# Two requests of 64 partitions in place of one with an outermost dimension of two, for the queries and keys of an attention head

## The chip, the cores and the metric

The kernel runs on one core of a Trainium2 chip. The metric is the device time of one execution in microseconds (us). The core has five engines with a queue of instructions each: PE (TensorE, the matrix products), DVE (VectorE), ACT (ScalarE), POOL (GpSimd) and SP (SyncE). A DMA request is an instruction in the queue of the engine that issues it, here SP or ACT; the bytes are then moved by the core's 16 DMA engines.

## The reference

One layer over 2048 latent tokens on a grid of 32 x 64 and 256 context tokens, width 1024. Shown is what the change touches: every latent query reads a window of 8 x 16 grid cells, with a learned bias, and all 256 context keys in one softmax.

```python
h_lat = _rmsnorm(x, norm_g[i]) * (1.0 + scale) + shift
na_q, na_k, na_v, na_g, r_q, r_k, r_v, r_g = _split_proj(h_lat @ w_in)
...
s_loc = jnp.einsum('bhrqd,bhrkd->bhrqk', qr, kg, preferred_element_type=jnp.float32) * scale + bias[None]
s_loc = jnp.where(mask, s_loc, -jnp.inf)
s_ctx = jnp.einsum('bhrqd,bhcd->bhrqc', qr, k_ctx, preferred_element_type=jnp.float32) * scale
p = jax.nn.softmax(jnp.concatenate([s_loc, s_ctx], axis=-1), axis=-1)
...
o = jnp.einsum('bhrqk,bhrkd->bhrqd', p_loc, vg) + jnp.einsum('bhrqc,bhcd->bhrqd', p_ctx, v_ctx)
```

There are 8 attention heads of width 64. Four retention heads of width 128 (a chunked recurrence in both directions) use the other columns of the projection. Both groups are gated, concatenated, projected by `w_out`, added to `x` and normalised.

## The kernel before

The products are made exact with pairs: a float32 tile is split into a high part `hi` (the reduced type that PE takes at speed) and a low part `lo`, and three products hi-hi, lo-hi and hi-lo are summed. That is why queries and keys exist twice in memory.

The work runs in four stages, in the order that the program writes out by hand for each engine.

1. Until about 165 us: normalisation of the tokens and projection of the attention keys. The keys of a pair of heads go to the DRAM tensor `kS`, with shape 128 x 2 x 2304 (64 rows for each head, the high and the low copy, the tokens).
2. Until about 597 us: the projections that are a list of jobs. `run_jobs` takes a block of 256 weight columns at a time and runs units over it. At the start of a job it splits the next job's weights (`w_parts`, ACT line 336, POOL line 338) and has SP load the weights after that (line 175). The value units `u_v` (nine for each of two jobs) copy a result of 256 tokens into a staging tile `o`, of which there are two, and store it into `vB` in eight requests of 24 or 32 partitions. The query units write `qS`, with shape 4 x 128 x 2 x 512 for each pair of heads: a block of 512 queries, 64 rows for each head, high and low copy.
3. Until about 1390 us: attention. A tile is a head with 128 queries; 8 heads with 4 blocks of 4 tiles make 128 tiles. The loop is a pipeline over four tiles: scores of tile t (`s_mm`, line 753, PE), normalisation of t-1, transposes of t-2 (`p_tr`), products with the values of t-3 (`pv`). Between these, `fill` deals out steps of the remaining projections, 318 of 384 over the loop, so that each tile gets between two and three.
4. The retention and the output projection.

Scores are computed with one instruction for 128 rows of the array: queries in rows 0 to 63 and the same queries again in rows 64 to 127, keys' high part in rows 0 to 63 and low part in rows 64 to 127. So both loads fill 128 partitions from 64 rows of memory. The query load repeats 64 rows twice; the key load takes the high and low copy from the middle dimension:

```python
for hl in range(2):
    nc.tensor.matmul(o, hd["q"][i][:, hl, j * P:(j + 1) * P], k, start=(hl == 0), stop=(hl == 1))
```

The query load (`load_q`, line 725) is issued by ACT, at the first tile of the block before; there are two query tiles. The key load (`load_head`, line 717) is issued by SP in the second block of the head before; there are two key tiles. Values (`load_v`, line 732), bias (line 737) and the weights of the filling projections (line 175) are SP's requests too, in the order of the program; a request whose buffer isn't free holds back those behind it. ACT also issues the gate loads (line 814) and all stores through `store`, which `defer` puts off until the next `tick`, the end of a unit or of a tile.

Of the kernel before, what the change touches and what calls it, by code (L numbers as in the profile page):

```python
# [81 lines left out]
def hybrid_kernel(ctx: ExitStack, tc: tile.TileContext, a: dict, out: bass.AP):  # L82
    nc = tc.nc
    f = lambda ap: ap[:].bitcast(F32)
# [3 lines left out]
    kS = [dram.tile([P, 2, LT], F32, name=f"kS{t}") for t in range(4)]  # L88
# [47 lines left out]
    def defer(n, fn):  # L136
        later.append([n, fn])
# [9 lines left out]
    def store(dst, src, n=1):  # L147
        q = env["queue"]
        defer(n, lambda: q.dma_start(dst, src))
# [211 lines left out]
    def tokform(w, tp):  # L361
        pm = ptile()
        for t in range(2):
            tk = 2 * tp + t
            (h1, h0), o = blk[tk // 4], (tk % 4) * P
            for k in range(KC):
                for i, (h, ww) in enumerate(((h1, w[0]), (h0, w[0]), (h1, w[1]))):
                    nc.tensor.matmul(pm[:, t * WG:(t + 1) * WG], h[:, k, o:o + P], ww[:, k, :],  # L368
                                     start=(k == 0 and i == 0), stop=(k == KC - 1 and i == 2))
                if k % 2 == 1:  # L370
                    yield
        return pm
# [45 lines left out]
    def u_v(w, c0, tp):  # L418
        pm = yield from tokform(w, tp)
        vt = op.tile([P, 2, 2, 2, P], F32R, name="o")  # L420
        pv = pm.rearrange("p (t h e d) -> p t h e d", t=2, h=2, e=2)
        for e in range(2):
            hs, ls = slice(64 * e, 64 * e + 64), slice(64 - 64 * e, 128 - 64 * e)
            nc.scalar.copy(vt[:, :, :, e, hs], pv[:, :, :, e, :])
            nc.vector.tensor_tensor(vt[:, :, :, e, ls], pv[:, :, :, e, :], f(vt)[:, :, :, e, hs], ALU.subtract)
        s, o = (c0 - 1024) // WG, f(vt).rearrange("p t h e d -> p t (h e d)")
        if tp == 8:
            store(vS[s].rearrange("(t p) h d -> p t (h d)", p=P), o)
            return
        for e, j in enumerate(VORD):  # L430
            k0, cw = CWIN[j]
            dst = vB[s][:4 * cw, tp, e, :].rearrange("(t r c) d -> r c t d", t=2, r=2)
            for r in range(2):
                store(dst[r], o[64 * r + k0:64 * r + k0 + cw])

    def put_tok(dstt, c0, tp, r, n=1):
        store(dstt[(c0 % 512) // WG][tp * 256:(tp + 1) * 256, :].rearrange("(t p) d -> p t d", p=P), r, n)
# [52 lines left out]
    run_acts(-1)  # L490

    jobs = [(1024, [(u_v, (tp,)) for tp in range(9)]), (1280, [(u_v, (tp,)) for tp in range(9)])]
    jobs += [(c0, [(u_gate, (ct, b)) for ct in range(2) for b in range(4)]) for c0 in (1536, 1792)]
    for n, (c0, u) in enumerate(((2560, u_rk), (2816, u_rk), (3072, u_rv), (3328, u_rv))):
# [219 lines left out]

    def load_head(h):
        k2 = kp.tile([P, LT], F32R, name="k2")
        nc.sync.dma_start(f(k2), kS[h // 2][64 * (h % 2):64 * (h % 2) + 64].rearrange("p e t -> e p t"))
        vc = kp.tile([P, 2, P], F32R, name="vc")
        nc.sync.dma_start(f(vc), vS[h // 4][:, h % 4, :].rearrange("(n p) d -> p n d", p=P))
        return dict(k2=k2, h=h, vc=vc, vt={}, q={})  # L720

    def load_q(hd, h, i):
        q = kp.tile([P, 2, 512], F32R, name="q", bufs=2)
        src = qS[h // 2][i, 64 * (h % 2):64 * (h % 2) + 64]
        nc.scalar.dma_start(f(q).rearrange("p e t -> p (e t)"), src.rearrange("p e t -> p (e t)").unsqueeze(0).to_broadcast([2, 64, 1024]))
        hd["q"][i] = q

    def load_v(hd, gs):
# [12 lines left out]
    def dims(t):  # L741
        h, i, j = t // 16, t // 4 % 4, t % 4
        return h, i, j, KWIN[i][0], KWIN[i][1], CWIN[j][0], CWIN[j][1]
# [90 lines left out]
    def run(n):  # L834
        for un in qu[n:n + 1]:
            for _ in un:
                pass
            tick()

    heads[0] = load_head(0)  # L840
    load_q(heads[0], 0, 0)
    load_v(heads[0], (0, 1, 2))
    for n in range(4):
# [118 lines left out]
    for t in range(NT + 3):  # L962
# [27 lines left out]
        h, i, j = dims(t)[:3]  # L990
# [7 lines left out]
        if i < 3 and j == 0:  # L998
            load_q(hd, h, i + 1)
        for g in {(0, 2): (3,), (0, 3): (4,), (1, 1): (5,), (1, 3): (6,), (2, 3): (7,)}.get((i, j), ()):  # L1000
            load_v(hd, (g,))
        if h + 1 < NH:
            if i == 1 and j == 2:
                heads[h + 1] = load_head(h + 1)
            if i == 3:
                nh = heads[h + 1]
                if j == 0:
                    load_q(nh, h + 1, 0)
                if j == 1:
                    bias(h + 1, 0, 0)  # L1010
                    load_v(nh, (0,))
                if j == 3:
                    bias(h + 1, 0, 1)
                    load_v(nh, (1, 2))
# [213 lines left out]
    q, r = divmod(48 - used, 7)  # L1228
    plan = [q + (n < r) for n in range(7)] + [15] * 8 + [10] * 4
    for s in range(NJ + 3):  # L1230
        q = plan[s]
# [121 lines left out]
```

## Time and profile before

| | us |
|---|---|
| median of 3 runs (lowest to highest) | 1728.46 (1726.64 to 1730.38) |
| the profiled execution, its own time | 1736.54 |
| its span, from the first to the last instruction | 1734.8 |
| PE busy, share of the span | 1410.3, 81% |
| DVE, ACT, POOL busy | 641.7, 530.2, 492.9 |
| mean granted clock of PE | 0.904 |
| moved by DMA | 270.44 MB, mean 156 GB/s |

The page divides the span into 40 slices and gives the busy share of each engine in tenths. A group of instructions is named by its line, engine, operation and `out<-in`; what ended an engine's idle time stands behind an arrow. "Granted clock" is the share of full speed that PE was given, and the DMA share is the mean busy share of the 16 DMA engines. A row of a stretch gives its bounds, its length, the busy time and count of PE, weight loads, DVE, ACT and POOL, the clock, the DMA share and the rate.

### The profile page before, as it was taken

What the parts mean: (1) busy time and instruction counts of PE and PEld (TensorE: products, weight loads), DVE (VectorE), ACT (ScalarE), POOL (GpSimd) and SP (SyncE); (2) the same over time, 40 slices, a digit from 0 to 9 for tenths busy, and PEclk for the clock granted to TensorE, in tenths of its full rate; (3) what the DMA queues carried; (4) which work ended last, traced back from release to release, by engine and by line L of the source; (5) the groups of instructions that cost most, each with busy time, mean ns of one, the idle gap of its engine ahead of it and who ended that gap; (6) DMA issues with size and microseconds to landing.
All of it is one profiled execution on the core that took longest, in us unless ns stands there. A gap on an engine that the chain in (4) does not pass through costs nothing. (4 is left out here: it accounts for less than half of the span.)

```text
span 1734.8 us, 22654 instructions
## 1 busy us (share of the span) xinstructions
PE 1410.3 (81%) x8380; PEld 1232.8 (71%) x8380; DVE 641.7 (37%) x1244; ACT 530.2 (31%) x1155; POOL 492.9 (28%) x499
## 2 busy tenths in 40 slices
PE   6999989999999537757574765738488998999998
PEld 2578988888788437756474765638378897988886
DVE  5782111001122114435342543426344444334445
ACT  4552112112222124333332322314244423343332
POOL 4433022012121113323222221213332323444442
PEclk9999989999999869878796887879788999999999
DMA  9435775124466423434242453534244389754643
GB/s 320 144 132 173 258 233 171 65 97 147 160 224 229 144 73 117 136 100 136 83 146 83 128 191 100 186 110 132 78 127 130 94 272 284 247 196 152 183 140 116
DMA packets 217505, 270.44 MB, mean 156 GB/s; under 512 B 15666, under 2 KB 162226, under 8 KB 216371
## 3 DMA queue, kind: packets, MB, share of 16 engines
q1 hardware_dynamic: 170386, 176.95, 32.9%
q10 hardware_dynamic: 47008, 92.03, 15.5%
q8 instruction: 67, 1.10, 0.3%
q14 instruction: 44, 0.35, 0.1%
HBM read 179.80 MB, written 89.13 MB: 155 GB/s over the span
## 5 line engine op out<-in xcount | busy, mean ns | idle before, releaser
L753 PE MATMUL sS<-k,q 128*128 128x256 f32 (+3 forms) x512 | 113.1, 348 | 223.2 <-DMA q<-qS 213.3
L357 PE MATMUL mm<-hhi,whi 128*128 128x512 f32 x640 | 264.3, 413 | 19.3 <-DVE o L387 17.4
L357 PE MATMUL mm<-hlo,whi 128*128 128x512 f32 x640 | 257.7, 403 | 5.8 <-DVE hlo L270 2.2
L753 PEld LDWEIGHTS sS<-k,q 128*128 128x128 f32 x512 | 94.2, 213 | 234.4 <-issue 224.2
L357 PE MATMUL mm<-hhi,wlo 128*128 128x512 f32 x640 | 257.7, 403 | 2.0 <-POOL wlo L338 1.7
L368 PE MATMUL mm<-whi,hhi 128*128 128x256 f32 x768 | 234.7, 306 | 6.0 <-ACT whi L336 6.0
L368 PE MATMUL mm<-wlo,hhi 128*128 128x256 f32 x768 | 225.6, 294 | 3.9 <-POOL wlo L338 3.9
L784 ACT CAST pt<-tr 128x640 fp32r<-128x640 f32 (+1 forms) x128 | 95.6, 747 | 433.1 <-PE tr L782 337.0
L368 PE MATMUL mm<-whi,hlo 128*128 128x256 f32 x768 | 224.8, 293 | 0.0
L338 POOL TENSOR_TENSOR wlo<-st,whi 128x256 fp32r<-128x256 f32 (+1 forms) x97 | 111.8, 1168 | 345.2 <-ACT whi L336 321.3
L773 POOL TENSOR_SCALAR sp<-sp,stt 128x640 f32<-128x640 f32 (+2 forms) x128 | 103.1, 807 | 328.0 <-DVE stt L772 271.0
L762 DVE CUSTOM_DVE_ANT_0 sp<-sS,nb 128x640 f32<-128x640 f32 (+2 forms) x128 | 105.6, 825 | 240.2 <-PE sS L753 207.7
L790 DVE TENSOR_TENSOR pt<-tr,pt 128x640 fp32r<-128x640 f32 (+1 forms) x128 | 113.9, 890 | 177.4 <-ACT pt L784 176.7
L368 PEld LDWEIGHTS mm<-whi,hhi 128*128 128x128 f32 x768 | 155.0, 202 | 6.2 <-ACT whi L336 6.2
L357 PEld LDWEIGHTS mm<-hhi,whi 128*128 128x128 f32 x640 | 123.4, 193 | 48.8 <-DVE o L387 17.9
L368 PEld LDWEIGHTS mm<-wlo,hhi 128*128 128x128 f32 x768 | 154.2, 201 | 4.6 <-POOL wlo L338 4.6
L368 PEld LDWEIGHTS mm<-whi,hlo 128*128 128x128 f32 x768 | 154.9, 202 | 0.0
L357 PEld LDWEIGHTS mm<-hlo,whi 128*128 128x128 f32 x640 | 123.3, 193 | 32.0 <-issue 3.2
L357 PEld LDWEIGHTS mm<-hhi,wlo 128*128 128x128 f32 x640 | 123.0, 192 | 32.3 <-POOL wlo L338 2.1
L767 ACT ACTIVATE sp<-sp,stt 128x640 f32<-128x640 f32 (+2 forms) x128 | 107.4, 839 | 15.6 <-DVE stt L762 15.4
L780 PE MATMUL tr<-ident,sp 128*128 128x128 f32 (+1 forms) x448 | 80.5, 303 | 29.9 <-DVE pt L790 29.7
L1197 PE MATMUL mm<-wor,y 128*128 128x512 f32 x384 | 95.9, 398 | 1.6 <-DVE xt L1206 0.7
(214 smaller groups left out, 2284.4 us busy)
## 6 DMA issues: line engine op xcount, KB each, us to landing
st<-in_w_in_dram SPq DMA_DIRECT2D x48, 512.0 KB
q<-qS ACTq DMA_DIRECT2D x32, 512.0 KB
k<-kS SPq DMA_DIRECT2D x8, 1152.0 KB
kS<-o SPq DMA_DIRECT2D x16, 512.0 KB
vB<-o ACTq DMA_DIRECT2D x64, 128.0 KB
woS<-g ACTq DMA_DIRECT2D x32, 256.0 KB
qS<-o ACTq DMA_DIRECT2D x16, 512.0 KB
vt<-vB SPq DMA_DIRECT2D x64, 128.0 KB
```

The lines of the kernel that those rows point to most:

```text
L338: eng.tensor_tensor(l, r, f(h), ALU.subtract)
L357: nc.tensor.matmul(pm[:, :n], ww[:, k, cs], h[:, k, :], start=(k == 0 and i == 0), stop=(k == KC - 1 and i == 2))
L368: nc.tensor.matmul(pm[:, t * WG:(t + 1) * WG], h[:, k, o:o + P], ww[:, k, :], start=(k == 0 and i == 0), stop=(k == KC - 1 and i == 2))
L753: nc.tensor.matmul(o, hd["q"][i][:, hl, j * P:(j + 1) * P], k, start=(hl == 0), stop=(hl == 1))
L762: nc.vector.tensor_tensor_reduce(T["sp"][:, :n], T["s"], nbz[big][:, o:o + n], -1.0, 3e38, ALU.add, ALU.min, T["st"][:, 0:1])
L767: nc.scalar.activation(sp[:, :n], sp[:, :n], AF.Exp, bias=st[:, 0:1], scale=-1.0, accum_out=st[:, 1:2])
L773: nc.gpsimd.tensor_scalar(sp[:, :n], sp[:, :n], st[:, 2:3], 0.0, ALU.mult, ALU.add)
L780: nc.tensor.transpose(tr[:cn, g, :], sp[:, T["lo"] + g * cn:T["lo"] + (g + 1) * cn], ident)
L784: nc.scalar.copy(pt[:, :ng_ + 2, 0, :], tr[:, :ng_ + 2, :])
L790: nc.vector.tensor_tensor(pt[:, :n, 1, :], tr[:, :n, :], f(pt)[:, :n, 0, :], ALU.subtract)
L1197: nc.tensor.matmul(pm, yy[:, k, :], ww[:, k, sl], start=(k == 0 and i == 0), stop=(k == 3 and i == 2))
```

## The change

Three places change. The keys of a head are loaded by two requests, one for the high copy into partitions 0 to 63, one for the low copy into partitions 64 to 127. The queries of a block are loaded by two requests of the same 64 rows, into the lower and the upper partitions. And of the eight stores of a value unit, the four of the second half of the partitions go to SP's queue in place of ACT's, one `tick` later than the others. The bytes and the destinations stay as they were.

```diff
@@ u_v
             dst = vB[s][:4 * cw, tp, e, :].rearrange("(t r c) d -> r c t d", t=2, r=2)
-            for r in range(2):
-                store(dst[r], o[64 * r + k0:64 * r + k0 + cw])
+            for r, q in enumerate((nc.scalar, nc.sync)):
+                defer(1 + r, lambda q=q, dst=dst[r], src=o[64 * r + k0:64 * r + k0 + cw]: q.dma_start(dst, src))
@@ load_head
-        nc.sync.dma_start(f(k2), kS[h // 2][64 * (h % 2):64 * (h % 2) + 64].rearrange("p e t -> e p t"))
+        for hl in range(2):
+            nc.sync.dma_start(f(k2)[64 * hl:64 * hl + 64, :], kS[h // 2][64 * (h % 2):64 * (h % 2) + 64, hl, :])
@@ load_q
         src = qS[h // 2][i, 64 * (h % 2):64 * (h % 2) + 64]
-        nc.scalar.dma_start(f(q).rearrange("p e t -> p (e t)"), src.rearrange("p e t -> p (e t)").unsqueeze(0).to_broadcast([2, 64, 1024]))
+        for e in range(2):
+            nc.scalar.dma_start(f(q)[64 * e:64 * e + 64], src)
```

## The prediction

> **What bounds the kernel now.** I read the page's slices first, then the stretches, the waits, the chain, and last single instructions. The slices (40 of 43.4 us; rows for TensorE, its granted clock and the DMA engines) show one stage that differs from the rest.
>
> ```profile
> PE   6999989999999537757574765738488998999998
> PEclk9999989999999869878796887879788999999999
> DMA  9435775124466423434242453534244389754643
> ```
>
> From the 14th to the 32nd slice TensorE is half idle, and the DMA engines are nowhere near full. That is the attention stage. Its stretch, beside one before it and one behind it (columns: length, then busy time of TensorE, weight loads, VectorE, ScalarE, GpSimd, then granted clock, DMA share, GB/s):
>
> ```profile
> 300.00:545.00 245.00, 245.00 (x1096) 198.79 (x1095) 32.73 (x30) 49.07 (x75) 43.56 (x27) 1.00 0.45 150
> 597.00:1390.00 793.00, 535.25 (x3586) 505.21 (x3586) 326.30 (x726) 261.61 (x547) 219.18 (x248) 0.82 0.38 120
> 1390.00:1480.00 90.00, 82.65 (x507) 72.21 (x506) 43.42 (x110) 26.89 (x57) 28.74 (x34) 0.96 0.89 278
> ```
>
> In attention TensorE is busy 535 of 793 us at a clock of 0.82, and no other engine passes 326 us. Something makes all of them wait. The waits name it (us in total, times, longest):
>
> ```profile
> PE sS L753 <- DMA q<-qS: 213.3, 27, 26.9
> DVE sp L762 <- PE sS L753: 207.7, 39, 28.1
> ```
>
> The scores wait for the queries, and VectorE for the scores. The chain of work that ended last gives the size of one such wait (start, us, what):
>
> ```profile
> 1130.77 37.37 DMA k<-kS
> ...
> 1284.57 14.23 DMA q<-qS
> 1298.94 1.24 PE sS L753 x4
> ...
> 1304.54 13.85 DMA q<-qS
> 1318.53 1.41 PE sS L753 x4
> ```
>
> A query block (512 KB) needs 14 us from issue to landing on a quiet machine, so it moves at about 37 GB/s; a head's keys (1152 KB) need 37 us, 31 GB/s. Blocks are issued only four tiles ahead. Is that the speed of memory? Three stretches answer (columns as above): two in which TensorE stands still for q, and one in which the only new requests are value stores of 24 or 32 partitions.
>
> ```profile
> 200.00:220.00 20.00, 20.00 (x172) 20.00 (x171) 2.97 (x7) 2.30 (x7) 0.00 (x0) 1.00 0.58 162
> 834.00:851.00 17.00, 0.00 (x0) 0.00 (x0) 0.00 (x0) 0.00 (x0) 2.24 (x3) 0.57 0.13 52
> 1242.00:1259.00 17.00, 0.00 (x0) 0.00 (x0) 0.16 (x1) 0.00 (x0) 1.71 (x3) 0.51 0.17 64
> ```
>
> While everybody waits, the share is 0.13: two of sixteen engines are 0.125. So the requests with an outermost dimension of two run on about two engines and the other fourteen rest. The small stores, whose outermost dimension is 24 or 32, hold a share of 0.58, more than nine engines' worth, and 162 GB/s.
>
> The Trainium skill says the same: in DMA: Bandwidth & Descriptors, Rules for kernel authors, an outermost dimension below 16, such as a broadcast of c copies in front, confines the request to at most c engines; the trace agrees, with 0.13.
>
> **The change part by part.** Queries and keys, attention stage. What the stage would take without these waits is read from tiles whose queries were already there: within a block, the second to the fourth tile. Starts of scores (start, us):
>
> ```profile
> 597.76 0.66 PE L753 MATMUL sS<-k,q 128*128 128x288 f32 x4
> 599.98 0.86 PE L753 MATMUL sS<-k,q 128*128 128x384 f32 x4
> ...
> 606.67 0.65 PE L753 MATMUL sS<-k,q 128*128 128x288 f32 x4
> ...
> 1179.02 0.75 PE L753 MATMUL sS<-k,q 128*128 128x384 f32 x4
> ...
> 1194.92 0.67 PE L753 MATMUL sS<-k,q 128*128 128x288 f32 x4
> ...
> 1366.16 0.76 PE L753 MATMUL sS<-k,q 128*128 128x384 f32 x4
> ...
> 1373.52 0.66 PE L753 MATMUL sS<-k,q 128*128 128x288 f32 x4
> ```
>
> From the first tile to the 128th it takes 1373.52 - 597.76 = 775.8 us, 6.1 us a tile. The 32 blocks give 64 intervals between second, third and fourth tile (first pair 599.98 to 606.67, last pair 1366.16 to 1373.52); without the one that holds the 37 us wait for keys, 63 intervals have a mean of 3.66 us. One block had its queries in time: four tiles from 1179.02 to 1194.92, 3.98 us each. I take 3.75, near the mean of the many, since the one block is a sample of four. The filling projections are dealt out evenly over the tiles, so the pace holds for all: 127 x 3.75 = 476 us. I add 10 for scattered waits, so 486 and a gain of 290 us.
>
> Bounds of that term: TensorE's own work is at least 535 x 0.82 = 439 us at full clock (an estimate from the stage's row; the clock of the 300 to 545 stretch shows that full occupancy is granted 1.00), a gain of 337. On the other side, 3.98 a tile gives 505, and if a wait of 2.2 us (an estimate, about a sixth of the 14 us) stays at each of 31 block changes, 573: a gain of 203.
>
> Does something else become late? The stage moves 793 us x 120 GB/s = 95 MB; in 486 us that is 196 GB/s, while 278 GB/s were moved at a share of 0.89 in the stretch from 1390. With the same packets the share becomes 0.38 x 793 / 486 = 0.62. VectorE becomes busy 326 / 486 = 67%, ScalarE 54% before its DMA issues. TensorE is next to be the bound, at about 90%. A 512 KB block at 162 GB/s needs 3.2 us, the keys 7 us, against a lead of four tiles, 15 us: hidden. If that cover were gone, each block would show its landing time less 15.
>
> More requests (issue times ns, min/median/max):
>
> ```profile
> L725 ACTq DMA_DIRECT2D q<-qS x32: 527/537/640, 558.1 to 1345.3; - x32
> L717 SPq DMA_DIRECT2D k<-kS x8: 510/511/661, 548.5 to 1223.1; - x8
> ```
>
> 32 more on ScalarE's queue at 0.54 are 17 us, eight more on SP's 4 us. What stands behind them on ScalarE are exponentials of a later tile; 17 us more on an engine that has 220 us free in 486 cost nothing that I can see. At worst all 17 come on the path, which keeps the gain at 186 or more.
>
> The entry to attention (ScalarE's copies of the last query projections):
>
> ```profile
> 556.37 0.59 ACT L386 CAST o<-mm 128x512 fp32r<-128x512 f32 x1 [5.01 <-PE mm L357]
> 561.97 0.59 ACT L386 CAST o<-mm 128x512 fp32r<-128x512 f32 x1 [5.01 <-PE mm L357]
> ...
> 589.20 0.58 ACT L386 CAST o<-mm 128x512 fp32r<-128x512 f32 x1 [26.64 <-DMA q<-qS]
> ```
>
> The units follow each other every 5.6 us until 561.97; then the queue stands for 26.6 us behind the first q and k. Three more units would put the last copy, and with it the first scores, at 561.97 + 3 x 5.6 = 578.8 in place of 597.8: 19 us. I take 18; between 0 (if bias and value loads take the place) and 19.
>
> The value stores. Half of them move from ScalarE's queue to SP's, one unit later. In the value projections ScalarE issues eight per unit:
>
> ```profile
> 173.93 12.02 ACTq L149 DMA_DIRECT2D vB<-o  x8
> ...
> 200.56 3.50 ACTq L149 DMA_DIRECT2D vB<-o  x8
> ...
> 222.52 3.50 ACTq L149 DMA_DIRECT2D vB<-o  x8
> ...
> 228.23 1.99 ACT L336 CAST whi<-st 128x1024 fp32r<-128x1024 f32 x2 [0.93 <-DVE o L425]
> ```
>
> From 200.56 to 222.52 four units take 5.49 us each on ScalarE; TensorE needs 48 x 20 / 172 = 5.58. ScalarE, thrown back by the first 12 us, therefore never catches up, and its next weight split at 228.23 is late. TensorE pays for it at both job changes:
>
> ```profile
> 229.33 0.58 PE L368 MATMUL mm<-whi,hhi 128*128 128x256 f32 x1 [6.00 <-ACT whi L336]
> 231.76 0.58 PE L368 MATMUL mm<-wlo,hhi 128*128 128x256 f32 x1 [1.63 <-POOL wlo L338]
> ...
> 292.21 0.50 PE L357 MATMUL mm<-hhi,whi 128*128 128x512 f32 x1 [1.89 <-ACT whi L336]
> 294.65 0.79 PE L357 MATMUL mm<-hhi,wlo 128*128 128x512 f32 x1 [1.71 <-POOL wlo L338]
> ```
>
> With four stores fewer, 1.75 us a unit, ScalarE regains 14 us over eight units and the 11.2 us of idling go nearly all. SP is free for it: it does nothing between these two rows but wait.
>
> ```profile
> 188.38 0.34 SPq L536 DMA_DIRECT2D hS<-hhi  x1
> ...
> 231.73 0.37 SPq L175 DMA_DIRECT2D st<-in_w_in_dram  x1
> ```
>
> Moved there, a store waits behind the spill stores and at worst behind a weight load; who waits then is the staging buffer's next writer on ScalarE, two units on. Bound for a loss: a weight load 3.5 us late at each of two changes, +7. I take -10, between +7 and -15.
>
> The tail behind 1390 is set by other loads (share 0.89) whose places in the program do not change: 0, plus or minus 5.
>
> **Sum.** -290 - 18 - 10 = -318 against the profiled execution's 1736.5 us (span 1734.8): 1418.5. The median of the runs shown lies 8.1 us below that execution, so 1410. The ends of all terms give -376 and -174 (the 17 us of issue among them), thus 1352 and 1554.
>
> **The rivals.** First, part of the wait stays: blocks land a little late at every change and the pace is that of the one full block. That is 573 us of attention, a gain of 203 + 18 + 10 = 231, time 1497. For it: the interval sample lies behind stalls that let the other engines catch up. Against it: 3.2 us of landing under a lead of 15.
>
> Second, the halves run one after the other and nothing is gained: queries land in 14 us as now, and the time stays near 1728, or 1718 with the value stores' part. Against it: the share of 0.13 beside 0.58 for requests of 24 and 32 partitions. The Trainium skill has this rule too, and it speaks against the change: DMA: Bandwidth & Descriptors, Rules for kernel authors, says not to bother with two transfers to disjoint partition halves, because both spray over all 16 engines and serialize. Its reason holds only where the one request already used all sixteen, which the 0.13 denies here.
>
> Third, on the other side: the 14 us are a price of the request, not of its bytes, and each half pays it in turn on ScalarE's queue. Then each of the 27 waits grows by 14: 27 x 14 = 378, time 2106. The point from which it decides is a half that lands no sooner than a whole does now. Against it: two engines' 52 GB/s over 14 us are 0.73 MB, so the bytes of the block with a little else account for the time.
>
> **How the numbers follow.** The forecast, TensorE the bound and 1375 to 1450, has 0.72; the first rival 0.23, the second 0.03, the third 0.02. The range 1375 to 1485 holds the forecast and roughly half of the first rival. Faster by over 0.2% (3.5 us, about what can be told from no change) is 0.95, within it 0.03, slower 0.02.
>
> **What would show it.** In the profile after: the wait of scores for q falls from 213 us to under 20; the stage's clock rises from 0.82 above 0.93, its DMA share from 0.38 to about 0.62; scores start every 3.7 to 3.9 us; first scores near 568 (18 and 10 earlier); no idle of 6 us at the first job change near 229. The prediction is wrong if scores still start in groups of four with a gap, if another load (values, weights, bias) takes the place of q among the waits, or if TensorE's busy time in the stage stays near 535.

## The result, and the profile after

The changed kernel takes 1403.15 us (median of 4 runs, 1399.77 to 1405.40) against 1727.55 us for the kernel before (median of 4). The ratio is 0.812, with a 95% interval of 0.810 to 0.814: 324 us less. The profiled execution took 1401.82 us with a span of 1400.0, 334.8 us below the span before. The code behind `load_head` moved by a line or two: the scores are line 755 now, the value stores line 434, the transposes 782 and 784.

The slices of the page, of 35 us each, in the order TensorE, granted clock, DMA engines:

```profile
PE   6999999999999999999999998899999999999997
PEclk9999999999999999999999999999999999999999
DMA  9543578743154678758768696966636898555533
```

The half-empty middle is gone, and the granted clock is nine tenths or more in every slice. The stretch of attention (length, busy time of TensorE, weight loads, VectorE, ScalarE, GpSimd, then clock, DMA share, GB/s), first and last scores, and the page's group of the scores with the idle time ahead of it:

```profile
565.00:1056.00 491.00, 473.73 (x3559) 449.62 (x3558) 325.15 (x726) 261.12 (x546) 219.35 (x248) 0.99 0.69 192
```

```profile
564.87 0.66 PE L755 MATMUL sS<-k,q 128*128 128x288 f32 x4
...
1042.29 0.66 PE L755 MATMUL sS<-k,q 128*128 128x288 f32 x4
```

```profile
L755 PE MATMUL sS<-k,q 128*128 128x256 f32 (+3 forms) x512 | 99.0, 315 | 4.6 <-DVE stt L764 4.2
```

From the first score to the start of the last tile's it takes 477.4 us in place of 775.8, 3.76 us a tile. TensorE is busy 96% of the stage. Ahead of the scores stand 4.6 us of idling, where 213 us were put down to the queries alone, and VectorE is what ended most of the 4.6.

ScalarE's row at the end of a value job, and the copy of a query projection just after the first query load, which stood at 561.97 before:

```profile
215.80 2.06 ACTq L434 DMA_DIRECT2D vB<-o  x4
...
221.93 2.00 ACT L336 CAST whi<-st 128x1024 fp32r<-128x1024 f32 x2 [0.93 <-DVE o L425]
...
548.26 0.59 ACT L386 CAST o<-mm 128x512 fp32r<-128x512 f32 x1 [5.01 <-PE mm L357]
```

What TensorE still waits for between 165 and 305 us is one line in the waits:

```profile
PE mm L368 <- POOL wlo L338: 2.7, 3, 1.3
```

The weight split starts at 221.9 in place of 228.2, the two waits of 6.00 and 1.89 us for it are gone, and the query units come 561.97 - 548.26 = 13.7 us earlier. In the changed kernel's execution TensorE had come into this stretch late: at 79 us, in code that the change does not touch, its matmuls were 2.4 us behind those of the execution before. The stretch itself therefore gave 16.1 us.

### The profile page after: what moved, and what is told of

It reads as the page before. It is cut to its first block, busy times and chain, and to the rows that moved or that the text cites. A ratio compares the mean times of both kernels' runs of the same rounds, so it can differ in the third digit from the quotient of the medians.

```text
span 1400.0 us, 22749 instructions
## 1 busy us (share of the span) xinstructions
PE 1346.2 (96%) x8380; PEld 1176.6 (84%) x8380; DVE 641.3 (46%) x1244; ACT 530.9 (38%) x1155; POOL 493.3 (35%) x499
## 3 DMA queue, kind: packets, MB, share of 16 engines
q10 hardware_dynamic: 43488, 84.69, 18.8%
## 4 chain that ended last, share of the span: by engine, by line
PE 77%; DMA 8%; DVE 6%; issue 3%; ACT 2%; POOL 2%; SPq 1%; ACTq 0%; POOLq 0%; DVEq 0%
PE mm L357 25%; PE mm L368 19%; PE mm L1199 12%; PE sS L755 4%; PE tr L782 3%; PE po L803 3%; PE mm L922 2%; PE mm L301 2%; PE tr L784 2%; PE po L805 1%; DMA q<-qS 1%; DMA hlo<-hS 1%; DMA vt<-vB 1%; DMA v<-rvS 1%; PE mm L1111 1%
## 5 line engine op out<-in xcount | busy, mean ns | idle before, releaser
L357 PE MATMUL mm<-hhi,whi 128*128 128x512 f32 x640 | 260.3, 407 | 0.0
L368 PE MATMUL mm<-whi,hhi 128*128 128x256 f32 x768 | 224.2, 292 | 0.0
L368 PE MATMUL mm<-wlo,hhi 128*128 128x256 f32 x768 | 216.7, 282 | 2.7 <-POOL wlo L338 2.7
L368 PE MATMUL mm<-whi,hlo 128*128 128x256 f32 x768 | 215.5, 281 | 0.0
L368 PEld LDWEIGHTS mm<-wlo,hhi 128*128 128x128 f32 x768 | 144.6, 188 | 3.4 <-POOL wlo L338 3.3
L368 PEld LDWEIGHTS mm<-whi,hlo 128*128 128x128 f32 x768 | 144.9, 189 | 0.0
L368 PEld LDWEIGHTS mm<-whi,hhi 128*128 128x128 f32 x768 | 144.8, 189 | 0.0
L755 PE MATMUL sS<-k,q 128*128 128x256 f32 (+3 forms) x512 | 99.0, 315 | 4.6 <-DVE stt L764 4.2
L755 PEld LDWEIGHTS sS<-k,q 128*128 128x128 f32 x512 | 83.8, 189 | 11.4 <-DVE stt L764 6.6
L1199 PE MATMUL mm<-won,y 128*128 128x512 f32 x336 | 89.9, 406 | 0.0
```

Of the source, the lines that this page charges most:

```text
L357: nc.tensor.matmul(pm[:, :n], ww[:, k, cs], h[:, k, :], start=(k == 0 and i == 0), stop=(k == KC - 1 and i == 2))
L1199: nc.tensor.matmul(pm, yy[:, k, :], ww[:, k, sl], start=(k == 0 and i == 0), stop=(k == 3 and i == 2))
```

## The experiments

Every kernel was timed beside runs of the kernel before on the same occasion; their medians were 1727.55 us for the changed kernel and 1729.0 to 1733.0 on the other occasions. The table gives the median, the ratio to the runs of the same occasion with its 95% interval, and from one profiled execution of each kernel the start of the first scores and the time from there to the last.

| kernel | us | ratio | first scores | scores, first to last |
|---|---|---|---|---|
| before | 1727.55 | 1 | 597.8 | 775.8 |
| changed | 1403.15 | 0.810 to 0.814 | 564.9 | 477.4 |
| queries alone | 1536.27 | 0.883 to 0.892 | 589.3 | 585.7 |
| keys alone | 1609.61 | 0.923 to 0.935 | 578.1 | 685.4 |
| queries and keys | 1417.36 | 0.814 to 0.822 | 581.8 | 477.5 |
| value stores alone | 1715.30 | 0.987 to 0.994 | 580.9 | 774.7 |
| outermost dimension 2 | 1790.64 | 1.027 to 1.038 | 577.9 | 853.8 |
| outermost dimension 4 | 1538.69 | 0.886 to 0.890 | 564.6 | 609.6 |
| outermost dimension 8 | 1438.88 | 0.830 to 0.833 | 562.3 | 514.6 |
| outermost dimension 16 | 1398.41 | 0.806 to 0.812 | 562.4 | 473.4 |
| one request, 128 rows | 1392.72 | 0.803 to 0.806 | 562.2 | 468.7 |
| two requests, 128 rows | 1400.36 | 0.807 to 0.813 | 562.4 | 478.4 |
| spaced reloads | 1394.29 | 0.804 to 0.809 | 564.6 | 469.7 |
| rows of each head's own | 1423.28 | 0.820 to 0.825 | 591.0 | 470.4 |

### The three parts alone

Queries alone: the edits of `load_head` and `u_v` are left out.

```diff
-        nc.scalar.dma_start(f(q).rearrange("p e t -> p (e t)"), src.rearrange("p e t -> p (e t)").unsqueeze(0).to_broadcast([2, 64, 1024]))
+        for e in range(2):
+            nc.scalar.dma_start(f(q)[64 * e:64 * e + 64], src)
```

> Only the queries are loaded in two requests of 64 partitions; keys and value stores as before. Theory A (a request with an outermost dimension of two runs on two DMA engines, and whatever queues behind it suffers): the queries' own waits go, but each of the keys' loads still holds two engines for some 37 us, and the values, bias and weights behind it on SP's queue, and two sixteenths of every query block, wait with it. In the trace before, the seven gaps in the block after a keys' load were 18 to 28 us longer than a plain tile, 158 us in sum; with that, 15 us of the entry and 14 us of the projections kept, 1590, range 1540 to 1610. Theory B (only the queries mattered, as the 213 us under their name suggest): about 1420.

Measured 1536: the keys did matter, as theory A has it and theory B has not, but by less than its sum, and the time lies just below its range. The chain of work that ended last names what remains (start, us, what):

```profile
545.07 33.27 DMA k<-kS
584.20 4.99 DMA vt<-vB
677.32 29.22 DMA k<-kS
760.51 21.09 DMA vt<-vB
820.04 32.68 DMA k<-kS
```

A head's keys still need about 30 us on their own, and a value load that stands behind them on SP's queue needs 21 us. The time from first to last score is 108 us longer than in the changed kernel, where 158 were expected.

Keys alone: only the edit of `load_head` is made.

```diff
-        nc.sync.dma_start(f(k2), kS[h // 2][64 * (h % 2):64 * (h % 2) + 64].rearrange("p e t -> e p t"))
+        for hl in range(2):
+            nc.sync.dma_start(f(k2)[64 * hl:64 * hl + 64, :], kS[h // 2][64 * (h % 2):64 * (h % 2) + 64, hl, :])
```

> Only the keys are loaded in two requests; queries and value stores as before. Theory A: every one of 32 blocks still waits until its queries have landed 14 us after their issue, a block of about 20 us in place of 15, 32 x 20 = 640 us of attention in place of 477: 1403 + 163 + 14 and some 10 at the entry, 1590, range 1550 to 1630. Theory B (the queries' 14 us were themselves caused by the keys' loads on the same two engines): the queries land sooner and the time falls below 1480.

Measured 1610, as theory A has it. Two of the query loads on the chain of that kernel, an early and a late one:

```profile
629.32 14.07 DMA q<-qS
...
1214.83 14.23 DMA q<-qS
```

With no keys on two engines in its way a query block still takes 14 us. The 14 us are its own.

Queries and keys, with all value stores on ScalarE; and value stores alone.

> Queries and keys in two requests, all value stores on ScalarE's queue as before. If the projections gain what the traces show (the last units 13.7 us earlier), this is 14 us slower than the changed kernel: 1417, range 1411 to 1421. If the earlier end of the projections had another cause than the stores, 1403.

> Only the value stores are divided between ScalarE's and SP's queue; queries and keys in one request as before. Expected 14 us below the kernel before: 1714, range 1708 to 1719. If the gain needs the other parts, or comes from another place, no change: 1727.

Without the division of the stores the time is 1417 (runs from 1410.8 to 1418.7, beside 1399.8 to 1405.4 of the changed kernel), with the division alone 1715. In attention neither differs from its neighbour: 477.5 beside 477.4, and 774.7 beside 775.8. The first scores come 16.9 us later in the one and 16.9 us earlier in the other, and that is where this part acts.

### Outermost dimension 2, 4, 8, 16 at the same number of requests

```diff
-            nc.scalar.dma_start(f(q)[64 * e:64 * e + 64], src)
+            nc.scalar.dma_start(f(q)[64 * e:64 * e + 64].rearrange("p e t -> p (e t)"), src.rearrange("(b a) e t -> a b (e t)", a=A))
```

The keys are dealt in the same way, `"(b a) t -> a b t"`.

> As the changed kernel, two requests each of 64 partitions, but the 64 rows on the memory side are dealt with an outermost dimension of 2 (row b*2+a, a outermost). The same rows of 4 and 9 KB, the same number of requests. The order of the 64 width components is permuted alike for queries and keys, so the scores are the same sums. Theory A (the outermost dimension sets how many DMA engines take part): two engines again, queries land 14 us and keys 37 us after issue, the time returns to that of the kernel before less the value stores' part, 1714, range 1700 to 1735. Theory B (the number or size of the requests matters): stays at 1403.

> As the last, with an outermost dimension of 4. Theory A: four engines, a query block lands in about 7 us, under the lead of four tiles or 15 us, and is hidden; a head's keys take 18 us, and what stands behind them on SP's queue waits a little: 1425, range 1403 to 1460. Theory B: 1403.

> As the last, with an outermost dimension of 8. Theory A: eight engines, a query block in 3.5 us and the keys in 9 us, all hidden: 1405, range 1400 to 1415. Theory B: 1403. This run gives the point from which more engines bring nothing.

> Control for the dealt rows: as with outermost dimensions of 2, 4 and 8, now 16. If only the number of DMA engines decides, all sixteen take part and the time is the changed kernel's 1403, range 1398 to 1410. If the dealing of the rows (other rows to each engine, other order) has a cost of its own, which would explain that 8 gave 1439 where 1405 was expected, it stays near 1430.

Two requests of 64 partitions bring nothing when their rows are dealt with an outermost dimension of two: 1791, even slower than before. With 4, 8 and 16 the same requests take 1539, 1439 and 1398, the last no slower than the changed kernel. So it is the outermost dimension that decides, and the dealing of the rows costs nothing by itself. The order of the 64 width components changes alike for queries and keys, so these kernels do the whole computation.

That the dimension acts through the number of DMA engines can be read from stretches in which TensorE stands still for these loads (columns as above, the DMA share last but one). One of each, with 2, 4 and 8 in this order:

```profile
1296.00:1312.00 16.00, 0.00 (x0) 0.00 (x0) 0.00 (x0) 0.00 (x0) 0.00 (x0) 0.50 0.13 46
```

```profile
828.00:835.00 7.00, 0.00 (x0) 0.00 (x0) 0.00 (x0) 0.00 (x0) 1.79 (x3) 0.75 0.28 92
```

```profile
655.00:660.00 5.00, 0.00 (x0) 0.00 (x0) 0.47 (x3) 0.00 (x0) 2.04 (x2) 0.73 0.63 139
```

Two, four and eight of sixteen are 0.125, 0.25 and 0.5; what the shares have above that is left for the other requests under way (in other such stretches they reach 0.23, 0.36 and 0.70). The Trainium skill's rule that an outermost dimension of c below 16 confines a request to at most c engines (DMA: Bandwidth & Descriptors, Rules for kernel authors) fits all three.

Query loads on the chains of the same three kernels, from the issue of the block's second request:

```profile
590.11 41.93 DMA q<-qS
...
1380.90 14.41 DMA q<-qS
```

```profile
575.18 23.30 DMA q<-qS
...
1018.58 9.63 DMA q<-qS
```

```profile
565.15 14.13 DMA q<-qS
```

Where no head's keys are under way, a block lands in 14.41 us with 2 and in 9.63 with 4. That is not half: other requests are under way too (the DMA share is 0.34 and 0.53 while they land), and some time passes before the first packet. The trace keeps every packet, and a block is 128 packets of 4096 bytes. From the issue of the first request to the end of the last packet the quickest block took 13.3, 8.1, 5.7 and 3.8 us with 2, 4, 8 and 16; in each case 1.3 to 1.4 us of that passed before the first packet began.

The first row of each fence shows what the expectations for 4 and 8 left out. It is a query load that met a head's keys (1152 KB, more than twice a block) under way. They expected 7 and 3.5 us, the size of a block alone; the load needed 23 and 14, against a lead of 15. The time from first to last score grew by 132 and by 37 us (609.6 and 514.6 less 477.4), where 22 and 2 were expected in all; the longest gaps before scores stand at the blocks after such loads. Hidden on average is not hidden behind the largest load.

That two requests dealt by two are 75 us slower than the value stores alone (1791 beside 1715) was not expected, and no run separates it. In the profiles the scores take 79 us longer (853.8 less 774.7), and some 55 of these stand at the blocks right behind a head's keys; the cause stays open.

### One request with 128 partitions outermost, or two

```diff
-        for e in range(2):
-            nc.scalar.dma_start(f(q)[64 * e:64 * e + 64], src)
+        nc.scalar.dma_start(f(q), qS[h // 2][i])
```

The keys come from `kS[h // 2][:, h % 2, :]` in one request. The second kernel reads the same rows by two requests of 64 partitions. Neither computes the layer: in place of the copies of one head's rows they read the rows of both heads of a pair, so the scores are other sums of the same size.

> One request again for each query block and for the keys, but with 128 partitions outermost on both sides: 128 different rows are read (both heads' rows of a pair, keys of one copy) in place of 64 rows in two copies, so the scores are other sums; bytes, rows and products are the same in size. Theory A: all sixteen engines, so the same as the changed kernel; 32 requests fewer on ScalarE take no time off the path: 1403, range 1396 to 1407. Rival (two requests of half the partitions serialize and cost their second start): faster than the changed kernel by up to 17 us, the issue time of 32 requests, 1386 to 1395.

> Two requests of 64 partitions for each query block and for the keys, as in the changed kernel, but over 128 different rows as in the kernel with one request of 128 (the scores are other sums). That one took 1392.7, 10 us less than the changed kernel. Theory C (the second request costs the 10 us, in issue or in landing): 1403, range 1399 to 1406. Theory D (reading the same 64 rows twice costs them): 1393, range 1389 to 1396.

One request took 1392.7, outside the range that the theory of sixteen engines had for it. With two requests over the same different rows it is 1400.4, and the intervals of the ratios (0.803 to 0.806 and 0.807 to 0.813) do not meet. So theory C holds against theory D: the second request has a price, about 8 us between these two kernels, and the doubly read rows have none that shows. Where it is paid can be read from the scores of the 75th and the 91st tile, first with two requests, then with one:

```profile
831.77 0.97 PE L755 MATMUL sS<-k,q 128*128 128x512 f32 x4 [0.21 <-DVE stt L764]
...
904.90 0.98 PE L755 MATMUL sS<-k,q 128*128 128x512 f32 x4 [1.62 <-DVE stt L764]
```

```profile
831.10 0.88 PE L753 MATMUL sS<-k,q 128*128 128x512 f32 x4
...
893.43 1.30 PE L753 MATMUL sS<-k,q 128*128 128x512 f32 x4 [2.03 <-DVE stt L762]
```

These sixteen tiles take 73.1 us with two requests and 62.3 with one. The 74 tiles ahead of them take 269.4 and 268.9, and those from the 91st to the last 135.8 and 137.4. The price is not paid at every block: it falls where the reloads of the next experiment are under way. The issue times are (ns, min/median/max), first of the two requests, then of the single one:

```profile
L727 ACTq DMA_DIRECT2D q<-qS x64: 452/456/712, 541.9 to 1019.0; - x64
```

```profile
L725 ACTq DMA_DIRECT2D q<-qS x32: 320/326/447, 541.7 to 1008.6; - x32
```

64 x 0.456 less 32 x 0.326 are 18.8 us of issue on ScalarE, spread over all 32 blocks. Outside the sixteen tiles none of it shows in the time, so the issue alone is not the price. The number of requests alone is not either: with an outermost dimension of 16, also two requests and dearer ones to issue (0.584 us), the same sixteen tiles take 67.0 us. What the second request does among the reloads, and whether it is that of the queries or of the keys, was not separated. The prediction had put the 17 us of added issue at nothing.

### Two attempts at a faster kernel

Spaced reloads, on the changed kernel. In the fifth and sixth head sixteen reloads of the activations come one filling step after the other, and here a step without a load is put ahead of each:

```diff
+                dmas.append(None)
                 dmas.append((f(blk[b][hl])[:, k:k + 2, :]...
```

> The changed kernel, with the sixteen reloads of the spilled activations in fifth and sixth head put on every second filling step in place of every step. In the trace after, the DMA share is 1.0 from 810 to 840 and from 870 to 900, and two intervals of tiles there are 9.65 and 8.47 us in place of 3.75, 11 us in sum. If these come from the bunched reloads, up to 10 us less: 1393 to 1400. If the sum of bytes in that time decides, no change: 1403.

Two intervals of tiles in the changed kernel, 9.65 and 8.47 us long, of the sixteen tiles just named:

```profile
838.23 0.75 PE L755 MATMUL sS<-k,q 128*128 128x384 f32 x4
847.88 1.04 PE L755 MATMUL sS<-k,q 128*128 128x288 f32 x4
...
885.55 0.97 PE L755 MATMUL sS<-k,q 128*128 128x512 f32 x4 [0.27 <-DVE stt L764]
894.02 0.74 PE L755 MATMUL sS<-k,q 128*128 128x384 f32 x4
```

With the reloads spaced the longest interval is 6.93 us, the sixteen tiles take 60.5 us in place of 72.5, the scores 469.7 in place of 477.4, and the time is 1394.3. The ratio's interval (0.804 to 0.809) lies just below that of the changed kernel (0.810 to 0.814). This is the fastest version here that does the whole computation.

Rows of each head's own, written twice for the queries, loaded by one request:

```diff
+        for e in range(2):
+            store(qS[2 * (c0 % 512 // P + ct) + e][b].rearrange("c p x -> p c x"),
+                  f(o)[64 * e:64 * e + 64].rearrange("p e t -> p (e t)").unsqueeze(1).to_broadcast([64, 2, 1024]))
...
+        nc.scalar.dma_start(f(q).rearrange("p e t -> p (e t)"), qS[h][i].rearrange("c p x -> (c p) x"))
```

> Whole computation. The copies are made on the way to memory: each head has its own tensor for keys (high rows, then low rows) and for queries (the same 64 rows written twice), by two store requests in place of one, with 64 partitions outermost; query block and keys are then loaded by one request with 128 partitions outermost. 8.4 MB more are written in the projections, where the DMA share is about 0.5, and 16 and 20 more stores are issued on ScalarE's and SP's queues there. If the second load request or the doubly read rows cost the 10 us, the time falls to 1393, range 1388 to 1400; if the projections pay for the stores, back to 1403 or above.

Attention gains its part (470.4), but the first scores start at 591.0, 26 us late. The stretches around the entry, of the changed kernel and then of this one, and the wait that holds TensorE in this one:

```profile
495.00:545.00 50.00, 50.00 (x216) 40.20 (x215) 14.69 (x17) 12.92 (x21) 13.20 (x13) 1.00 0.78 265
545.00:580.00 35.00, 33.85 (x198) 29.53 (x197) 9.17 (x21) 12.47 (x26) 8.68 (x12) 1.00 0.85 242
```

```profile
495.00:545.00 50.00, 50.00 (x216) 40.18 (x215) 12.42 (x14) 10.45 (x17) 11.83 (x12) 1.00 0.93 279
545.00:580.00 35.00, 10.56 (x40) 8.16 (x39) 3.46 (x5) 2.34 (x4) 0.00 (x0) 0.65 0.96 307
```

```profile
577.08 0.79 PE L357 MATMUL mm<-hhi,whi 128*128 128x512 f32 x1 [24.44 <-DVE o L388]
```

The expectation took the DMA share of the whole stage, about 0.5. The doubled stores fall into its last 100 us, where the share was 0.78 and 0.85 already; it went to 0.93 and 0.96. The waits put 35.9 us of ScalarE's waiting between 540 and 590 us down to value loads and to the stores of the staging tiles, and TensorE waited 24 us for a copy into one. That the doubled bytes cause this, and not the greater number of store requests, was not separated.

## Why the prediction was right

The prediction was 1410 us in a range of 1375 to 1485, the measured time 1403. By its steps, in the spans of the two profiled executions (334.8 us apart, 318 forecast):

- **Attention, -290.** Measured 775.8 - 477.4 = 298. The mechanism was right; that the pace fits so closely is in part luck. 3.75 us lay between the 63 intervals' mean of 3.66 and the one block's 3.98, and it became 3.76 with all waits in it. The first 64 tiles took 3.65 us each, as the 63 intervals have it, and the sixteen tiles among the reloads took some 14 us more than that pace. So the pace of 3.75 was a little too slow, and the waits, nearly all in one place, are larger than the 10 us put down for them; the two errors partly cancel. The bound of a 337 us gain lay too far: in 565 to 1056 us TensorE is busy 473.7 us at a clock of 0.99, not 439. The stage's mean clock of 0.82 that gave 439 counts the idle time too, where the clock stands at 0.51 to 0.57 in the two rows of the prediction.
- **The entry, -18.** First scores came 32.9 us earlier, at 564.9, of which 13.7 are the projections' part, so 19.2. The three units followed at 5.6 us each, as the rows before said. (The prediction's own terms of 18 and 10 give first scores at 569.8; its 568 was a slip.)
- **Value stores, -10.** 13.7 at the query units, 16.1 in the stretch itself. ScalarE regained its place and both waits for the weight split went, as described; nearly all of the 11.2 us of waits went, and the rest fits the clock, which the sum had left out: between 295.7 and 301.1 us the matmuls of the execution before fell back by another 2.2 us without a wait. The stretch from 165 to 305 us before and after (columns as above; the clock stands third from the end):

```profile
165.00:305.00 140.00, 127.60 (x993) 124.15 (x994) 15.70 (x37) 25.00 (x50) 26.19 (x12) 0.94 0.71 224
```

```profile
165.00:305.00 140.00, 137.33 (x1063) 132.45 (x1062) 16.15 (x38) 27.82 (x55) 28.36 (x12) 1.00 0.74 233
```

   The two kernels that separate this part agree: 14 us slower than the changed kernel without it, and 16 us faster with it alone than the kernel before on the same occasion (1731.7).
- **The tail, 0.** From last scores to the end it is 357.7 in place of 361.3, 3.6 us less.
- **The extra requests, nothing.** This step failed in the small: one request in place of two saves about 8 us. It is not the issue time that the prediction weighed, since the saving falls in sixteen tiles alone.
- **The first rival** (part of the wait stays) was not so for sixteen engines. With eight or four a wait stays, but above all at the blocks behind a head's keys and not at every change.
- **The second and third rival.** The halves do not serialize in the sense that would have left the time at 1728, and the 14 us were no price of the request, since the same two requests end at quickest after 13.3 us or after 3.8 with the outermost dimension alone changed from 2 to 16. The Trainium skill's rule against two transfers to disjoint halves (DMA: Bandwidth & Descriptors, Rules for kernel authors) fits where its reason holds: beside one request that already takes all sixteen, two are 8 us slower here.

The DMA share was forecast at 0.62 and became 0.69, at 192 GB/s where 196 were forecast.

## What to carry to other kernels

When an engine waits for a load while the DMA share of that stretch stands near a small multiple of a sixteenth, look at the outermost dimension of the load on both sides: a dimension of two in front, a broadcast or a high and a low copy, used about two engines of sixteen here. Read the gain from the pace of the pieces that did not wait, not from the sum of the waits. And price a lead by the largest load that is under way with it, and an added transfer by the share in the very stretch where it falls, not by an average.

## What the runs showed of the hardware

While TensorE stood still for loads with an outermost dimension of 2, 4 and 8, the DMA share was 0.13, 0.28 and 0.63 in the three stretches shown. A query block of 512 KB ended at quickest 13.3, 8.1, 5.7 and 3.8 us after its first issue with 2, 4, 8 and 16. For a query load, a request of 64 partitions and 256 KB cost 0.456 us to issue (0.476 in the changed kernel), one of 128 partitions and 512 KB 0.326, and the one of 512 KB with an outermost dimension of two 0.537: of the two requests for the same 512 KB, the one with 128 partitions outermost was the cheaper. Where sixteen engines took part, two requests in place of one showed in the time only among reloads that took the DMA share to 1.0. Two requests dealt by two over the same bytes were slower than one, 1791 beside 1715 us, which stays open.
